# Sums of squares behind the output projection of a hybrid encoder layer: three whole token tiles per square, and a square root read from PSUM

## The chip, the cores and the metric

The kernel runs on 1 core of one Trainium2 chip. The metric is the device time of one execution in microseconds (us); the median of several runs is compared. Engines are named as in the profile: PE is TensorE, PEld its weight load, DVE VectorE, ACT ScalarE, POOL GpSimd, SP SyncE.

## The reference, cut to what matters

One layer with four token mixers and a gated feed-forward net over 272 tokens (16 meta tokens and 256 real ones) of width 2048, in float32. The stretch around the change is the norm behind the output projection:

```python
def rms_norm(x, g):
    xf = x.astype(jnp.float32)
    y = xf * lax.rsqrt(jnp.mean(xf * xf, axis=-1, keepdims=True) + EPS)
    return (y * g.astype(jnp.float32)).astype(x.dtype)
...
    mix = jnp.concatenate([y_a, y_b, y_c, y_d], axis=-1) @ w_out
    x = x + rms_norm(mix, g_mix_post)
    h = rms_norm(x, g_ffn_pre)
    gate = causal_dwconv(h @ ffn_w_gate, ffn_conv_w, ffn_conv_b)
    y = (jax.nn.silu(gate) * (h @ ffn_w_up)) @ ffn_w_down
    return x + rms_norm(y, g_ffn_post)
```

## The kernel before

Activations lie with features on the partitions and tokens along the free dimension. From the output projection on, 258 tokens are kept (2 that the causal convolution of the feed-forward net needs, and 256 real ones), cut into three segments by `SEGQ`: 2, 128 and 128 tokens. Every float32 weight tile is loaded from HBM by SP into one of three `raw` buffers, then split in halves of 128x1024 into a high part (`whi`, ACT, L176) and a low part (`wlo`, DVE, L182); a product is three matmuls (high by high, high by low, low by high: L237, L238, L239).

The output projection (L983 to L1012) makes 16 feature tiles in four groups of four. When a feature tile is done, ACT squares it from its PSUM bank and DVE adds the square to `ssum` (L964 to L970), and DVE multiplies it by the norm's gain into `mo` (`weigh`, L1001). The square of the last feature tile is not added: it stays apart as `slast` (L1005).

Then, from L1013 on, a stretch follows in which DVE and ACT run in the order in which their instructions are written (`manual_schedule`, L1014). PE is not held so: a list scheduler orders PE's instructions when the kernel is built, by its own idea of when operands are ready. `pin` (L107) ties one instruction behind the one that was written just before it for the same engine; it doesn't tie what is written later. The stretch is, in the order of writing:

- Line 1015 takes a PSUM bank `mrstd`, out of the pool `mx` with four banks.
- Lines 1017 and 1018: a quarter-wise split of a weight tile (`pieces`): four ACT copies, and the first of four DVE subtractions.
- Line 1019 calls `rstd_columns` (L271 to L286). It calls `square_sums` (L263 to L269): for `ssum`, then for `slast`, one matmul per segment (segments in the order 1, 2, 0) with the squares as the weights and a column of ones as the moving operand, so that the sums of 128, 128 and 2 tokens land as columns of a second bank of `mx`; 6 calls of matmul. Then POOL's memset of the tile `rs`, two DVE instructions that read the bank and compute mean + EPS (L283 for the segment of two tokens, L284 for the two of 128), and `rsqrt` (L288 to L296): ACT takes the root (L290), meanwhile DVE does one more subtraction of `pieces`, then the reciprocal (L293) and one Newton step (L294 to L296). Column `y` of the result is the reciprocal root, tokens on partitions.
- Line 1020: the remaining two subtractions of `pieces`.
- Lines 1057 to 1063: 32 PE transposes of `mo` (eight groups of four, `turned`, L1047 to L1051), each group into a bank of `mx`, the first five groups read by an ACT copy each (`keep`, L1054); in between, behind the fourth group, three PE transposes (`rstd_spread`, L298 to L299) that spread `y` along the tokens into `mrstd`.
- Lines 1065 to 1087: per feature tile k, DVE multiplies `mo` by `mrstd` (L1066), adds it to the residual stream (L1067), and ACT and DVE make the high and low part of the norm's input `hx` (L1070, L1071). The feed-forward matmuls begin with `hx` of feature tile 0.

Of the kernel before, what the change touches and what calls it, by code (L numbers as in the profile page):

```python
# [7 lines left out]
F32 = mybir.dt.float32  # L8
F32R = mybir.dt.float32r
AF = mybir.ActivationFunctionType  # L10
ALU = mybir.AluOpType
AX = mybir.AxisListType

P = 128
# [4 lines left out]
D = 2048  # L19
# [5 lines left out]
EPS = 1e-6  # L25
# [24 lines left out]
SEGQ = ((0, 2), (2, 128), (130, 128))  # L50
# [43 lines left out]
def hybrid_layer(ctx: ExitStack, tc, t):  # L94
    nc = tc.nc
    mm = nc.tensor.matmul
    act = nc.scalar.activation
    V = nc.vector
    G = nc.gpsimd

    const = ctx.enter_context(tc.tile_pool(name="const", bufs=1))
# [5 lines left out]
    pin = tc.keep_in_program_order  # L107
# [4 lines left out]
    def mix_ps():  # L112
        return pmix.tile([P, 512], F32, tag="mx", name="mx")
# [5 lines left out]
    sel_fox, sel_ssd, sel_tok = (cst[0:16, c:c + P] for c in (C_SELFOX, C_SELSSD, C_SELTOK))  # L119
    ones = const.tile([P, P], F32, name="ones")  # L120
    V.memset(ones, 1.0)

    def col(c):
        return cols[:, c:c + 1]
# [39 lines left out]
    def split_hi(i, half, n, pool=None, tiles=None):  # L164

        load(i)
        hi, lo = tiles or [(pool or wpool).tile([P, 1024], F32R, tag=tag, bufs=4, name=tag) for tag in ("whi", "wlo")]
        halves[i, half] = (hi, lo)
        steps = []
        cuts = [1024 * q // n for q in range(n + 1)] if (i, half) != (0, 0) else [0, 128, 512, 1024]  # L170
        for c in map(slice, cuts, cuts[1:]):
            if i:
                src = raws[i][:, 1024 * half + c.start:1024 * half + c.stop]
            else:
                src = packed(FIRST_W[2 * half + c.start // 512] + c.start % 512, c.stop - c.start)
            act(hi[:, c], src, AF.Copy)  # L176
            steps.append((lo[:, c], src, hi[:, c].bitcast(F32)))
        return iter(steps)

    def split_lo(steps, most=None):  # L180
        for _, (lo, src, hi) in zip(range(most or 16), steps):
            V.tensor_tensor(lo, src, hi, ALU.subtract)  # L182
# [80 lines left out]
    def square_sums(sq, segs, ps, g):  # L263
        n_seg = len(segs)
        order = [(j, i) for j in range(len(sq[g])) for i in (1, 2, 0)]
        for j, i in order:
            c0, n = segs[i]
            mm(ps[0:n, g * n_seg + i:g * n_seg + i + 1], sq[g][j][:, c0:c0 + n], ones[:, 0:1],
               start=g == 0 and (j, i) == order[0], stop=(j == len(sq[g]) - 1), skip_group_check=True)  # L269

    def rstd_columns(small, sq, scale, segs, ps, meanwhile=None, summed=False):  # L271

        n_seg, ng = len(segs), len(sq)
        if not summed:
            for g in range(ng):
                square_sums(sq, segs, ps, g)
        w = ng * n_seg
        v = small.tile([P, 4, 8], F32, tag="rs", bufs=2, name="rs")
        G.memset(v, 1.0)
        n0 = segs[0][1]  # L280
        pv = ps[:, 0:w].rearrange("p (g s) -> p g s", g=ng)
        vv = v[:, 0, 0:w].rearrange("p (g s) -> p g s", g=ng)
        V.tensor_scalar(vv[0:n0, :, 0:1], pv[0:n0, :, 0:1], scale, EPS, op0=ALU.mult, op1=ALU.add)  # L283
        V.tensor_scalar(vv[:, :, 1:n_seg], pv[:, :, 1:n_seg], scale, EPS, op0=ALU.mult, op1=ALU.add)  # L284
        rsqrt(v[:, 0, 0:w], v[:, 1, 0:w], v[:, 2, 0:w], v[:, 3, 0:w], meanwhile)
        return v[:, 2, 0:w]  # L286

    def rsqrt(v, s, y, z, meanwhile=None):  # L288

        pin(act(s, v, AF.Sqrt))  # L290
        if meanwhile:
            meanwhile()
        V.reciprocal(y, s)  # L293
        V.tensor_tensor(z, y, y, ALU.mult)  # L294
        V.scalar_tensor_tensor(z, z, -0.5, v, op0=ALU.mult, op1=ALU.mult)
        V.scalar_tensor_tensor(y, z, 1.5, y, op0=ALU.add, op1=ALU.mult)  # L296
# [661 lines left out]
    T = tst.enter_context(tc.tile_pool(name="resid", bufs=1, side="right"))  # L958
# [3 lines left out]
    ssum = T.tile([P, LQ], F32, name="ssum")  # L962
# [20 lines left out]
    for f4 in range(4):  # L983
# [13 lines left out]
        for f in range(4):  # L997
# [5 lines left out]
            if k == KT - 1:  # L1003
                slast = T.tile([P, LQ], F32, tag="tsq", bufs=2, name="slast")
# [11 lines left out]

    pieces = split_hi(FFN0 + 2, 0, 4)
    split_lo(pieces, 1)
    y = rstd_columns(T, [[ssum, slast]], 1.0 / D, SEGQ, mix_ps(), lambda: split_lo(pieces, 1))
    split_lo(pieces)  # L1020
    assert "early" in finished
    mixers.close()
# [175 lines left out]
    for k in range(FT):  # L1198
        i = base + k
# [28 lines left out]
    for b in range(2):  # L1228
# [20 lines left out]
        s, y, z = (st[:, c:c + 1] for c in (8, 9, 10))  # L1249
# [8 lines left out]
        if b:  # L1258
# [3 lines left out]
            for i, ps in enumerate(sums):  # L1262
                c0 = n_v + 256 * i
# [86 lines left out]
```

## Time and profile before

| | |
|---|---|
| median of 3 runs | 1126.2 us (1126.0 to 1126.65) |
| profiled execution, its own time | 1126.16 us |
| profiled execution, span from first to last instruction | 1124.0 us |
| PE busy | 1117.2 us |
| DVE busy | 721.9 us |
| ACT busy | 556.8 us |
| POOL busy | 30.9 us |
| mean granted PE clock | 0.999 of full speed |

The profile is of one execution. Busy time of PE counts matmuls whose ends are modelled, so that short waits between them can hide in it. A releaser (`<-`) is what ended an idle stretch. The span is 2.16 us shorter than the time of the same execution; that remainder lies outside the instructions.

### The profile page before, as it was taken

How to read it: one execution, taken by the hardware profiler on the slowest of the kernel's cores; microseconds unless marked ns; L12 is line 12 of the kernel's file. 1: busy time of each engine (PE TensorE's matmuls, PEld its weight loads, DVE VectorE, ACT ScalarE, POOL GpSimd, SP SyncE). 2: the span in 40 equal slices, each digit the busy share in tenths (PEclk: the TensorE clock that was granted, in tenths of full speed). 3: DMA queues.
4: the chain of work that ended last, by engine and by line, in shares of the span. 5: the costliest groups of instructions: out<-in, count | busy, mean ns of one | idle time of the engine just before them, and what ended most of it. 6: DMA issues, size and time to landing. Idle time of an engine off the chain costs nothing.

```text
span 1124.0 us, 18509 instructions
## 1 busy us (share of the span) xinstructions
PE 1117.2 (99%) x7590; PEld 1024.2 (91%) x7590; DVE 721.9 (64%) x1177; ACT 556.8 (50%) x820; POOL 30.9 (3%) x45
## 2 busy tenths in 40 slices
PE   9999999999999999999999999999999999999998
PEld 8999999999999999999899899998999888888886
DVE  7686676786656977656656566566665654455564
ACT  8343464573444656445444454445444544444453
POOL 0000011000000400000000000000000000000000
PEclk9999999999999999999999999999999999999999
DMA  9744434535556465555455545555555555555552
GB/s 322 254 168 173 153 132 160 170 141 178 185 180 214 183 220 193 187 186 184 157 203 183 183 180 190 185 188 187 188 187 187 188 187 191 192 201 200 190 187 75
DMA packets 32724, 208.30 MB, mean 185 GB/s; under 512 B 3696, under 2 KB 4736, under 8 KB 9344
## 3 DMA queue, kind: packets, MB, share of 16 engines
q1 hardware_dynamic: 30528, 198.17, 49.5%
q0 software_dynamic: 1680, 8.56, 2.3%
q8 instruction: 59, 0.97, 0.3%
q10 hardware_dynamic: 432, 0.39, 0.1%
q14 instruction: 25, 0.20, 0.0%
HBM read 204.99 MB, written 2.12 MB: 184 GB/s over the span
## 4 chain that ended last, share of the span: by engine, by line
PE 98%; DVE 1%; DMA 0%; ACT 0%; issue 0%; SPq 0%; DVEq 0%
PE acc L237 16%; PE acc L239 16%; PE acc L238 16%; PE mx L232 15%; PE mx L233 7%; PE acc L1194 4%; PE acc L1195 4%; PE acc L1193 4%; PE mx L1194 3%; PE mx L1195 3%; PE mx L1193 3%; PE mx L1226 1%; PE mx L620 1%; PE mx L237 1%; PE mx L238 1%; PE mx L239 1%
## 5 line engine op out<-in xcount | busy, mean ns | idle before, releaser
L182 DVE TENSOR_TENSOR wlo<-raw,whi 128x1024 fp32r<-128x1024 f32 (+2 forms) x369 | 445.4, 1212 | 321.4 <-ACT whi L176 315.5
L176 ACT ACTIVATE whi<-raw 128x1024 fp32r<-128x1024 f32 (+2 forms) x369 | 383.3, 1047 | 450.1 <-PE acc L238 194.5
L232 PE MATMUL mx<-hx,whi 128*128 128x512 f32 x704 | 249.2, 397 | 0.0
L233 PE MATMUL mx<-hx,wlo 128*128 128x256 f32 x704 | 197.7, 281 | 0.0
L239 PE MATMUL acc<-hx,wlo 128*128 128x258 f32 x688 | 195.0, 284 | 0.0
L238 PE MATMUL acc<-hx,whi 128*128 128x258 f32 x688 | 193.8, 282 | 0.0
L237 PE MATMUL acc<-hx,whi 128*128 128x258 f32 x688 | 193.1, 283 | 0.0
L232 PEld LDWEIGHTS mx<-hx,whi 128*128 128x128 f32 x704 | 132.5, 188 | 31.8
L237 PE MATMUL acc<-xh,whi 128*128 128x272 f32 (+3 forms) x512 | 151.5, 298 | 0.6 <-ACT whi L176 0.6
L238 PE MATMUL acc<-xl,whi 128*128 128x272 f32 (+3 forms) x512 | 146.6, 287 | 0.0
L239 PE MATMUL acc<-xh,wlo 128*128 128x272 f32 (+3 forms) x512 | 145.2, 287 | 0.4 <-DVE wlo L182 0.4
L233 PEld LDWEIGHTS mx<-hx,wlo 128*128 128x128 f32 x704 | 132.5, 188 | 0.0
L238 PEld LDWEIGHTS acc<-hx,whi 128*128 128x128 f32 x688 | 130.2, 189 | 0.3 <-DVE hx L1071 0.2
L237 PEld LDWEIGHTS acc<-hx,whi 128*128 128x128 f32 x688 | 129.7, 189 | 0.6
L239 PEld LDWEIGHTS acc<-hx,wlo 128*128 128x128 f32 x688 | 129.5, 188 | 0.0
L237 PEld LDWEIGHTS acc<-xh,whi 128*128 128x128 f32 x512 | 96.6, 189 | 7.2 <-issue 5.0
L238 PEld LDWEIGHTS acc<-xl,whi 128*128 128x128 f32 x512 | 96.9, 189 | 1.2 <-issue 0.7
L239 PEld LDWEIGHTS acc<-xh,wlo 128*128 128x128 f32 x512 | 95.8, 189 | 0.9 <-DVE wlo L182 0.9
L1195 PE MATMUL acc<-wlo,yh 128*128 128x512 f32 x176 | 68.5, 389 | 0.0
L1194 PE MATMUL acc<-whi,yl 128*128 128x512 f32 x176 | 68.5, 389 | 0.0
L1193 PE MATMUL acc<-whi,yh 128*128 128x512 f32 x176 | 68.5, 389 | 0.0
L1193 PE MATMUL mx<-whi,yh 128*128 128x512 f32 x160 | 62.2, 389 | 0.0
(379 smaller groups left out, 1499.3 us busy)
## 6 DMA issues: line engine op xcount, KB each, us to landing
raw<-w_gate SPq DMA_DIRECT2D x44, 1024.0 KB, 4.8
raw<-w_up SPq DMA_DIRECT2D x44, 1024.0 KB, 4.7
raw<-w_down SPq DMA_DIRECT2D x44, 1024.0 KB, 4.8
raw<-w_in SPq DMA_DIRECT2D x32, 1024.0 KB, 4.9
raw<-w_out SPq DMA_DIRECT2D x16, 1024.0 KB, 4.9
xT<-xT POOLq DMA_DIRECT2D x1, 2064.0 KB, 12.0
raw<-w_in SPq DMA_DIRECT2D x4, 512.0 KB, 7.8
yT<-x_tok POOLq DMA_DIRECT2D x1, 2048.0 KB, 8.1
```

Of the source, the lines that this page charges most:

```text
L176: act(hi[:, c], src, AF.Copy)
L182: V.tensor_tensor(lo, src, hi, ALU.subtract)
L232: mm(accs[f][:, :2 * n], hi[:, c], both(kts[k]), start=st, stop=False)
L233: mm(accs[f][:, n:2 * n], lo[:, c], xh, start=False, stop=en)
L237: mm(out, hi[:, c], xh[:, o:], start=st, stop=False)
L238: mm(out, hi[:, c], xl[:, o:], start=False, stop=False)
L239: mm(out, lo[:, c], xh[:, o:], start=False, stop=en)
L620: mm(ps[:, j * nk:(j + 1) * nk], q[r, h0 // 2 + j, qc:qc + P], k[r, h0 // 2 + j, 0:nk], start=True, stop=True)
L1193: mm(o, yh, hi[:, c], start=(k == 0), stop=False)
L1194: mm(o, yl, hi[:, c], start=False, stop=False)
L1195: mm(o, yh, lo[:, c], start=False, stop=(k == FT - 1))
L1226: mm(po[1][q], y, w[:, c], start=False, stop=(k == FT - 1 and w is lo))
```

## The change

A tile `eps` of one column is set to EPS at the start. Behind the output projection the call of `rstd_columns` is replaced: the sums are taken over three tiles of 128 tokens that begin at tokens 0, 2 and 130 (the first overlaps the second; of its result only the first two tokens are used), first the three of `ssum`, then the three of `slast`, each matmul pinned behind the one before it. ACT takes the root directly from the bank of the sums, with `eps` as its bias and 1/D as its scale; one DVE instruction writes mean + EPS for the Newton step. The tile `rs` is no longer set on POOL beforehand. The remaining uses of `rstd_columns` are as they were.

```diff
     ones = const.tile([P, P], F32, name="ones")
     V.memset(ones, 1.0)
+    eps = const.tile([P, 1], F32, name="eps")
+    V.memset(eps, EPS)
...
     pieces = split_hi(FFN0 + 2, 0, 4)
     split_lo(pieces, 1)
-    y = rstd_columns(T, [[ssum, slast]], 1.0 / D, SEGQ, mix_ps(), lambda: split_lo(pieces, 1))
+
+    psq = mix_ps()
+    for sq in (ssum, slast):
+        for i, c0 in enumerate((0, 2, 130)):
+            pin(mm(psq[:, i:i + 1], sq[:, c0:c0 + P], ones[:, 0:1], start=(i == 0 and sq is ssum),
+                   stop=sq is slast, skip_group_check=True))
+    v = T.tile([P, 4, 3], F32, tag="rs", name="rs")
+    s, y, z = (v[:, i, :] for i in (1, 2, 3))
+    pin(act(s, psq[:, 0:3], AF.Sqrt, bias=eps, scale=1.0 / D))
+    V.tensor_scalar(v[:, 0, :], psq[:, 0:3], 1.0 / D, EPS, op0=ALU.mult, op1=ALU.add)
+    split_lo(pieces, 1)
+    V.reciprocal(y, s)
+    V.tensor_tensor(z, y, y, ALU.mult)
+    V.scalar_tensor_tensor(z, z, -0.5, v[:, 0, :], op0=ALU.mult, op1=ALU.mult)
+    V.scalar_tensor_tensor(y, z, 1.5, y, op0=ALU.add, op1=ALU.mult)
     split_lo(pieces)
```

## Rows read from the trace of the kernel before

**Rows 1.** The page: its span, and busy time, share and instructions of each engine.
```profile
span 1124.0 us, 18509 instructions
...
PE   1117.2 (99%) x7590; PEld 1024.2 (91%) x7590; DVE 721.9 (64%) x1177; ACT 556.8 (50%) x820; POOL 30.9 (3%) x45
```

**Rows 2.** All waits of PE in the span: in total, times, longest (us).
```profile
PE mx L358 <- DVE ones L121: 1.1, 1, 1.1
PE acc L237 <- ACT whi L176: 0.6, 1, 0.6
PE acc L239 <- DVE wlo L182: 0.4, 2, 0.2
PE mx L299 <- DVE rs L296: 0.2, 1, 0.2
```

**Rows 3.** By stretch: length, busy time (count) of PE, PEld, DVE, ACT, POOL, clock, DMA.
```profile
366.60:372.20 5.60, 5.39 (x51) 5.02 (x49) 4.30 (x16) 4.25 (x11) 0.56 (x1) 1.00 0.82 293
...
420.00:800.00 380.00, 380.00 (x2684) 356.25 (x2683) 240.50 (x347) 186.05 (x245) 0.00 (x0) 1.00 0.53 186
```

**Rows 4.** Chain of work that ended last, in order of time: start, length, what.
```profile
370.07 0.55 PE mx L299 x3
370.62 1.78 PE mx L1050 x16
```

**Rows 5.** Timeline of PE's weight loads: start, length, line, out<-in, count [idle before].
```profile
366.61 0.63 PEld L268 LDWEIGHTS mx<-ones,ssum 128*128 128x128 f32 x6
367.28 0.53 PEld L1050 LDWEIGHTS mx<-cst,mo 128*128 128x128 f32 x5
367.77 0.63 PEld L268 LDWEIGHTS mx<-ones,slast 128*128 128x128 f32 x6
368.44 1.19 PEld L1050 LDWEIGHTS mx<-cst,mo 128*128 128x128 f32 x11
370.04 0.34 PEld L299 LDWEIGHTS mx<-cst,rs 2*128 2x128 f32 x3 [0.42 <-issue]
...
372.14 0.53 PEld L237 LDWEIGHTS acc<-hx,whi 128*128 128x128 f32 x4
```

**Rows 6.** One line's instructions: ns shortest, median and longest, first and last start, forms.
```profile
L268 PEld LDWEIGHTS mx<-ones,slast x6: 81/191/192, 367.8 to 368.3; 128*128 128x128 f32 x4, 128*2 128x2 f32 x2
```

**Rows 7.** Timeline of ACT in the stretch of the change.
```profile
367.03 0.37 ACT L1005 ACTIVATE slast<-acc 128x258 f32<-128x258 f32 x1
...
368.92 0.20 ACT L290 ACTIVATE rs<-rs 128x3 f32<-128x3 f32 x1 [1.22 <-DVE rs L284]
369.03 2.66 ACT L1054 ACTIVATE xtok<-mx 128x512 f32<-128x512 f32 x5
371.58 0.50 ACT L1070 ACTIVATE hx<-xT,cols 128x258 fp32r<-128x258 f32 x1
```

**Rows 8.** Timeline of DVE in the stretch of the change.
```profile
367.43 0.48 DVE L1001 TENSOR_SCALAR mo<-acc,cols 128x258 f32<-128x258 f32 x1 [0.36 <-ACT slast L1005]
368.62 0.15 DVE L283 TENSOR_SCALAR rs<-mx 2x1 f32<-2x1 f32 x1 [0.70 <-PE mx L268]
...
368.76 0.40 DVE L182 TENSOR_TENSOR wlo<-raw,whi 128x256 fp32r<-128x256 f32 x1
369.16 0.18 DVE L293 RECIPROCAL rs<-rs 128x3 f32<-128x3 f32 x1
...
369.76 0.16 DVE L296 SCALAR_TENSOR_TENSOR rs<-rs 128x3 f32<-128x3 f32 x1
369.84 0.75 DVE L182 TENSOR_TENSOR wlo<-raw,whi 128x256 fp32r<-128x256 f32 x2
370.65 0.42 DVE L1066 TENSOR_TENSOR mo<-mo,mx 128x258 f32<-128x258 f32 x1
```

**Rows 9.** ACT by line and shape, 1100 to 1124 us: count, busy, mean ns.
```profile
L1250 ACT ACTIVATE fst<-fst 128x1 f32<-128x1 f32 x2 | 0.6, 296 | 0.0
```

**Rows 10.** Timeline of DVE at the start of the kernel.
```profile
3.19 0.36 DVE L375 TENSOR_SCALAR xh<-first 128x272 fp32r<-128x272 f32 x1 [1.99 <-DMA first<-first]
```

## The prediction

> **What bounds the kernel now.** I read the page's engine shares first: PE is busy 1117.2 us of a span of 1124.0 us, so a gain can only come out of PE's work or out of PE's few idle moments [rows 1]. All waits of PE that the profile names come to 2.3 us, and one of them, L299 waiting for the end of the Newton step, lies in the stretch of the change [rows 2]. The table by stretch says the same: between 366.6 and 372.2 us PE lacks 0.21 us of being always busy, and in the long feed-forward stretch from 420 to 800 us it lacks nothing, DMA at 0.53 of its share [rows 3]. So whatever moves the first feed-forward matmul at 372.14 us [rows 5] is carried unchanged to the end: nothing behind it has slack to swallow a shift or a wait for weights to undo it.
>
> The stretch itself is read in three timelines side by side. PE: six sums of `ssum` from 366.61, five transposes from 367.28, six sums of `slast` from 367.77, eleven transposes from 368.44, then 0.42 us without a weight load before the three spreads of `y` at 370.04 [rows 5]. DVE: the bank is read at 368.62, reciprocal at 369.16, last Newton step from 369.76 to 369.92, and the first product with the spread root at 370.65 [rows 8]. ACT: `slast` from 367.03 to 367.40, root at 368.92, five copies in a row until 371.69, overlapping by a little the first `hx` at 371.58 [rows 7]. The spreads wait for the Newton step, not for PE: the path is slast, its sums, root, reciprocal, Newton, spreads (370.07 plus 0.55), the 16 transposes behind them, feed-forward [rows 4]. From the load of the first spread to the first feed-forward load it is 2.10 us, filled twice over: by PE's transposes (until 372.40 in the chain) and by the product, the sum and `hx`, which ends at 372.08 [rows 4, 5, 7]. So a gain counts only if it reaches the spreads, and there it counts one to one.
>
> **Part 1: three sums in place of six, twice.** Six loads of `ssum` take 367.28 − 366.61 = 0.67 us, 0.11 us each [rows 5]. Three fewer ahead let PE go on at 366.95. What comes next is not in the diff: the pin holds each sum behind the previous one, but transposes, written later and not pinned, may still be listed in between, as five of them are now. Five take 0.49 us, 0.10 us each [rows 5]. With n of them, the first sum of `slast` loads at 366.95 + 0.10 n, and not before `slast` is there. That ends at 367.40 [rows 7]; from the end of the last Newton step at 369.92 to the spreads' load it is 0.12 us [rows 5, 8], so I take 367.52. Up to n = 5 the wait decides; n = 6 gives 367.55, n = 8 gives 367.75, hardly earlier than now. More than 8 don't fit: `mx` has four banks, one each for `mrstd` and the sums, and two groups of four fill the others.
>
> Now the bank is read 368.62 − 367.77 = 0.85 us after the first load [rows 5, 8]. Three sums fewer take away 0.33, leaving 0.52; but the last one is now a whole tile, whose load takes 0.19 us where that of two tokens takes 0.08 [rows 6], so 0.52 to 0.63, and I take 0.60. The sums are then readable at 368.12 to 368.15 (n up to 6) or 368.35 (n = 8): 0.47 to 0.50, or 0.27 us, sooner. I have no row that says which n the list takes; three sums of 0.11 us are three transposes' worth of room more than now, which points from 5 towards 8, so I take 6 to 8.
>
> **Part 2: the root from the bank.** The two DVE instructions ahead of the root go off the root's path, which starts 0.30 us after the sums now (368.62 to 368.92) [rows 7, 8]. But the root was not what the reciprocal waited for: it ends at 369.12, and DVE reaches the reciprocal at 369.16 straight from the subtraction of 0.40 us at 368.76 [rows 7, 8]. The reciprocal stands 0.54 us behind the first read of the bank, by DVE's own work.
>
> The new DVE instruction, mean + EPS, reads the same bank as the root. Two readers of one bank are ordered here: L1001 on DVE and L1005 on ACT both only read the last accumulator, and L1001 sat 0.36 us until L1005 was over, starting 0.03 us behind it [rows 7, 8]. The root is written first, so DVE waits for it. Behind the waiting instruction on DVE stand the subtraction of 0.40 us and then the reciprocal. The root's price is not in the trace: without bias and scale operands it is 0.20 us [rows 7], with a bias tile, at the end of the kernel, 0.296 us [rows 9]. The second is nearest, since `eps` is a tile. So from the sums to the reciprocal: 0.30 root, 0.03 until DVE starts, 0.07 for mean + EPS (the spacing of the two that it replaces, 0.14 us for two), 0.40 subtraction: 0.80 us in place of 0.54, that is 0.26 us later [rows 7 to 9]. With the root at 0.20 us it is 0.16 us later.
>
> [...] If both could read at once, the reciprocal would stand 0.47 us behind the sums and the whole would be 0.33 us better than my sum. [...]
>
> **The rest.** The setting of `eps` falls on DVE before 3.19 us, where DVE waits 1.99 us for the first DMA [rows 10]; nothing. The dropped memset is on POOL, busy 3% [rows 1]; nothing. The root now frees ACT for its copies earlier than 369.03 [rows 7], and they are then paced by the transposes; ACT is not late. The two subtractions behind the Newton step end at 370.59 now, 0.03 us ahead of the spreads [rows 4, 8]; they move with the Newton step. The subtractions also free a weight buffer for SP's next load; that moves by the same tenths, and PE waits for no load behind this point [rows 2]. If PE idles a little longer ahead of `slast`, the clock is no worry that rows show: 0.42 us of idle in this stretch left it at 1.00 [rows 3, 5].
>
> **The sum.** For n up to 6: 0.47 to 0.50 sooner, 0.26 later, net 0.21 to 0.24 us gained. For n = 8: 0.27 − 0.26, nothing. In between, 0.15 us. With the profiled execution's own time of 1126.16 us that is 1126.0; it stands 0.04 us under the median of 1126.2, so the median becomes 1126.05, rounded to 1126.0.
>
> **Rivals.**
> First, a clearer gain: DVE does not wait for the root, or the root is short. For: ACT sat 1.22 us idle ahead of the root, so nothing there can hold it up [rows 7]. Against: L1001's wait. Without the wait the gain is 0.33 + 0.22 = 0.55 us, with a root of 0.20 us it is 0.32: 1125.6 to 1125.9.
>
> Second, slower: the spreads are listed behind more transposes. They stand behind 16 of 32 now, and PE idles before them [rows 5], because the fifth group's bank comes free only with ACT's copies. With the root earlier by 368.92 − 368.15 = 0.77 us, these copies, some 0.53 us apart (2.66 for five) [rows 7], free banks sooner, and a list that fills idle room may put two more groups ahead of the spreads. The fifth group needs the end of the second copy, about 369.5, the sixth that of the third, about 370.05; eight transposes then end near 370.5, and the spreads load there in place of 370.04: 0.46 us slower, 1126.6. One group more ends near 369.95 and gives 1126.1. It decides from the second extra group on. Against: only if the list expects `y` later than it now does.
>
> Third, the change doesn't do what it says: the sums end up no earlier, with n = 8 and one more wait, or the list of PE comes out otherwise somewhere else. In the first form it is 0 to 0.1 us slower, 1126.2 to 1126.3. In the second nothing here prices it; what speaks against it is that before this stretch only a memset of a column is new and behind it PE is full [rows 3].
>
> **How the numbers follow.** The forecast 0.55 (1125.9 to 1126.25), the clear gain 0.18, the slower spreads 0.15, the third 0.12. The range reaches from the clear gain to the slower spreads, with the 0.2 to 0.45 us by which single runs lie under and over the median (1126.0 to 1126.65): 1125.3 to 1126.8. Bounds for faster and slower are 0.2%, 2.25 us, about what a measurement of this kernel can tell from no change; all worked-out cases are inside, and only a list that changes elsewhere could leave it: 0.03 faster, 0.94 same, 0.03 slower.
>
> **What would show it.** In the timeline of PE: three sums, some transposes, three sums, each sum 0.11 us apart. On ACT the root at 368.1 to 368.4 with a length near 0.30 us. On DVE mean + EPS behind the root's end, waiting for ACT, and the reciprocal about 0.80 us behind the root's start. The first feed-forward load at 371.9 to 372.1, and the same shift in the span. It is wrong if mean + EPS starts with the root (then 0.33 us better), if the spreads load later than 370.04, or if the span moves by more than 1 us, since no part of this stretch holds that much.

## The result: 1132.11 us, 5.9 us slower, and where the time went

The changed kernel takes 1132.11 us (1131.97 to 1132.25, five runs) against 1126.2 us (1126.0 to 1126.65): a ratio of 1.0052, 95% interval 1.0041 to 1.0063. The forecast was 1126.0 us with a range up to 1126.8.

The page of the changed kernel, its span and engine shares, answers to [rows 1]:

```profile
span 1130.5 us, 18504 instructions
...
PE 1123.2 (99%) x7590; PEld 1023.3 (91%) x7590; DVE 722.5 (64%) x1177; ACT 557.2 (49%) x820; POOL 30.4 (3%) x44
```

PE has the same 7590 matmul rows as before and is busy 6.0 us longer, while its named waits grow only from 2.3 us [rows 2] to 2.9 us: the matmuls themselves stand further apart. Since the rows are the same in number and, from stage to stage, in kind, the two traces can be laid beside each other matmul by matmul. In the table below the stages are cut at the starts of five matmuls: the first sum of `ssum`, the first feed-forward matmul, the first and the last matmul of the down projection, and the last matmul of the kernel. The numbers are differences of those starts in us.

```
                         first sum at  the stretch  gate and up  down     behind it
before                   366.73        5.43         503.65       239.50   3.95
with the change          366.34        5.63         503.65       246.11   3.94
```

The stretch that the change is about loses 0.20 us. Gate and up projection take the same to the hundredth. The down projection, of which the diff says nothing, loses 6.61 us. The stages up to the first sum are 0.39 us shorter; that start lay between 366.16 and 366.99 us in the runs of the longer table below.

The view by stretch, first two lines of the kernel before, then two of the changed one (stretch, its length, busy time and count of PE, PEld, DVE, ACT, POOL, granted clock, DMA share, GB/s):

```profile
500.00:800.00 300.00, 300.00 (x2111) 280.87 (x2110) 186.55 (x265) 143.58 (x186) 0.00 (x0) 1.00 0.52 183
950.00:1000.00 50.00, 50.00 (x222) 41.42 (x221) 26.21 (x28) 22.31 (x28) 0.00 (x0) 1.00 0.55 192
```

```profile
500.00:800.00 300.00, 300.00 (x2111) 280.95 (x2110) 186.71 (x266) 143.59 (x186) 0.00 (x0) 1.00 0.52 183
950.00:1000.00 50.00, 50.00 (x216) 40.13 (x216) 24.67 (x28) 21.69 (x27) 0.00 (x0) 1.00 0.54 190
```

PE is busy for the whole of each stretch in both, at the same clock of 1.00. What differs is the count: 2111 against 2111 in the gate and up projections, but 222 against 216 in 50 us of the down projection. "Busy" hides it; the count in brackets shows it.

Four matmuls in a row there, PE's timeline, first of the kernel before, then of the changed one:

```profile
950.39 0.39 PE L1195 MATMUL mx<-wlo,yh 128*128 128x512 f32 x1
950.62 0.39 PE L1193 MATMUL mx<-whi,yh 128*128 128x512 f32 x1
950.84 0.39 PE L1194 MATMUL mx<-whi,yl 128*128 128x512 f32 x1
951.07 0.39 PE L1195 MATMUL mx<-wlo,yh 128*128 128x512 f32 x1
```

```profile
950.28 0.40 PE L1211 MATMUL acc<-wlo,yh 128*128 128x512 f32 x1
950.52 0.39 PE L1209 MATMUL acc<-whi,yh 128*128 128x512 f32 x1
950.75 0.40 PE L1210 MATMUL acc<-whi,yl 128*128 128x512 f32 x1
950.98 0.39 PE L1211 MATMUL acc<-wlo,yh 128*128 128x512 f32 x1
```

From start to start it is 226.7 ns before and 233.3 ns after, as means over 960 matmuls; 1056 matmuls times 6.6 ns is 7.0 us, of which 6.6 appear, since the last 96 stepped unevenly already before.

The stretch itself, timelines of PEld, ACT and DVE of the changed kernel, answering to [rows 5, 7, 8]:

```profile
366.22 0.75 PEld L1025 LDWEIGHTS mx<-ones,ssum 128*128 128x128 f32 x6
366.81 0.62 PEld L1066 LDWEIGHTS mx<-cst,mo 128*128 128x128 f32 x5
367.40 0.75 PEld L1025 LDWEIGHTS mx<-ones,slast 128*128 128x128 f32 x6
367.98 1.27 PEld L1066 LDWEIGHTS mx<-cst,mo 128*128 128x128 f32 x11
369.85 0.33 PEld L301 LDWEIGHTS mx<-cst,rs 2*128 2x128 f32 x3 [0.60 <-ACT xtok L1070]
...
371.95 0.53 PEld L239 LDWEIGHTS acc<-hx,whi 128*128 128x128 f32 x4
```

```profile
368.27 0.26 ACT L1029 ACTIVATE rs<-mx,eps 128x3 f32<-128x3 f32 x1 [0.95 <-PE mx L1025]
```

```profile
368.56 0.16 DVE L1030 TENSOR_SCALAR rs<-mx 128x3 f32<-128x3 f32 x1 [1.04 <-ACT rs L1029]
368.64 0.42 DVE L184 TENSOR_TENSOR wlo<-raw,whi 128x256 fp32r<-128x256 f32 x1
368.97 0.17 DVE L1032 RECIPROCAL rs<-rs 128x3 f32<-128x3 f32 x1
...
369.57 0.16 DVE L1035 SCALAR_TENSOR_TENSOR rs<-rs 128x3 f32<-128x3 f32 x1
...
370.47 0.42 DVE L1082 TENSOR_TENSOR mo<-mo,mx 128x258 f32<-128x258 f32 x1
```

Two things are to be seen. Each square still has six loads and five transposes still stand between: three sums of a float32 square are six rows, before and after, and nothing was taken off PE. And mean + EPS waits 1.04 us, in the end for ACT's root, from the start of which the reciprocal is 0.70 us away (368.27 to 368.97).

### The profile page after: what moved, and what is told of

Read it like the earlier page. It is cut to its first block, busy times and chain, and to the rows that moved or that the text cites. A ratio compares the mean times of both kernels' runs of the same rounds, so it can differ in the third digit from the quotient of the medians.

```text
span 1130.5 us, 18504 instructions
## 1 busy us (share of the span) xinstructions
PE 1123.2 (99%) x7590; PEld 1023.3 (91%) x7590; DVE 722.5 (64%) x1177; ACT 557.2 (49%) x820; POOL 30.4 (3%) x44
## 4 chain that ended last, share of the span: by engine, by line
PE 98%; DVE 0%; DMA 0%; ACT 0%; issue 0%; SPq 0%
PE acc L239 16%; PE acc L241 16%; PE acc L240 16%; PE mx L234 15%; PE mx L235 7%; PE acc L1210 4%; PE acc L1209 4%; PE acc L1211 4%; PE mx L1210 3%; PE mx L1209 3%; PE mx L1211 3%; PE mx L1242 1%; PE mx L622 1%; PE mx L239 1%; PE mx L241 1%; PE mx L240 1%
```

## The experiments

The suspect came from the diff itself: `eps` is a new tile. It holds one column, but it stands in the pool `const` and takes 32 bytes of every partition there, and all pools allocated behind `const` from the same side move by 32 bytes: `raw`, `whi`, `wlo` and the activations that stand on that side, `hx` among them. `yh` and `yl`, at the other end of the memory, don't move. In the built kernels `whi` begins at byte 37344 of the partition before and at 37376 after, `yh` at 219104 in both. In the down projection `whi` and `wlo` are the moving operands and `yh` and `yl` the weights, so their distance changes by 32 bytes.

**The tile and the code, taken apart.** First the change without the move:

```diff
-    eps = const.tile([P, 1], F32, name="eps")
+    root_eps = const.tile([P, 2], F32, name="root")
+    root, eps = root_eps[:, 0:1], root_eps[:, 1:2]
     V.memset(eps, EPS)
...
-    root = const.tile([P, 1], F32, name="root")
```

> The change as it is, but eps is the second column of the tile root, which already has 32 bytes, so that no other tile moves. Theory 'place' (the 6.6 us come from the 32 bytes by which the new tile eps moves all tiles behind it, the split weights whi and wlo among them, while yh and yl stay where they were): a matmul of the down projection steps every 226.7 ns again in place of 233.3 ns, and the time falls to that of the kernel before plus the 0.2 us that the stretch of the change loses, 1126.2 to 1126.6 us. Rival 'code' (the new sums or the root from the bank do it): 233.3 ns and 1132 us as with the change.

Then the move without the change, on the kernel before:

```diff
     V.memset(ones, 1.0)
+    pad = const.tile([P, 8], F32, name="pad")
+    V.memset(pad, EPS)
```

> The kernel before with nothing but an unused tile of 32 bytes behind ones, set once. Theory 'place': 233.3 ns per down matmul, 1131.6 to 1132.1 us. Rival 'code': 226.7 ns and 1126.2 us.

Measured: 1126.26 us with eps in root, a ratio of 1.000 to the kernel before (0.999 to 1.001), and 1132.33 us with the unused tile, 1.0054 (1.0037 to 1.0071). The stretch from 950 to 1000 us, first with eps in root, then with the unused tile:

```profile
950.00:1000.00 50.00, 50.00 (x222) 41.42 (x221) 26.21 (x28) 21.87 (x27) 0.00 (x0) 1.00 0.55 193
```

```profile
950.00:1000.00 50.00, 50.00 (x216) 40.17 (x215) 24.68 (x28) 21.83 (x27) 0.00 (x0) 1.00 0.53 190
```

The 222 and 216 matmuls go with the tile and not with the code: the step is 226.7 ns in the first run and 233.3 ns in the second. What the diff means to do is worth nothing that the times can tell, and the whole loss that they can tell is made by 32 bytes of room. "Place" stands, "code" falls.

**Place or distance.** Does it count where `whi` lies, for instance on a multiple of 64 bytes, or how far it lies from the weights? The tile made 64 bytes long:

```diff
-    eps = const.tile([P, 1], F32, name="eps")
+    eps = const.tile([P, 16], F32, name="eps")[:, 0:1]
```

> The change with eps as a tile of 64 bytes, so that tiles move by 64 in place of 32 bytes. If what counts is whether whi and wlo begin on a multiple of 64 bytes (32 beyond one is fast, on one is slow): 226.7 ns, 1126.4 us. If it is the distance in bytes between the moving operand and the weights over a longer period: another step than 226.7, somewhere between 226 and 240 ns, 1126 to 1139 us.

And `yh`, `yl` moved alone, in the kernel before, by another distance at each step k:

```diff
-        yh = Y.tile([P, SEQ], F32R, tag="yh", bufs=LAST + 1, name="yh")
-        yl = Y.tile([P, SEQ], F32R, tag="yl", bufs=LAST + 1, name="yl")
+        o = 8 * (k % 16)
+        yh = Y.tile([P, SEQ + P], F32R, tag="yh", bufs=LAST + 1, name="yh")[:, o:o + SEQ]
+        yl = Y.tile([P, SEQ + P], F32R, tag="yl", bufs=LAST + 1, name="yl")[:, o:o + SEQ]
```

> The kernel before with yh and yl placed 32*(k mod 16) bytes into longer tiles, k being the step of the down projection; whi and wlo stay. If the distance between moving operand and weights counts, the step of the matmuls goes with k mod 16: 226.7 ns at 0, 233.3 ns at 15 (the distance that the change has), others between. If only the place of the moving operand counts: 226.7 ns for every k and 1126.2 us.

Measured: 64 bytes give 1128.63 us (1.0022, interval 1.0012 to 1.0031) and 228.9 ns: neither the old step nor the worse one, so a multiple of 64 is not the rule. The view by stretch of that run:

```profile
950.00:1000.00 50.00, 50.00 (x220) 41.02 (x219) 25.67 (x29) 21.83 (x27) 0.00 (x0) 1.00 0.54 190
```

With the moved weights (1131.6 us, one run) the step follows k mod 16. Mean start-to-start of the matmuls within a step k of the down projection, k = 1 to 39; the two or three k of the same offset agree within 0.1 ns:

```
yh, yl moved by (bytes)   0     32    64    96    128   160   192   224
step (ns)                 226.7 233.1 233.4 233.9 233.5 233.4 229.3 233.3
moved by                  256   288   320   352   384   416   448   480
step (ns)                 226.7 233.1 233.4 233.9 233.5 233.4 229.3 233.3
```

The pattern repeats after 256 bytes. Moving the weights by 224 is the same distance as moving the operand by 32 (233.3 ns both), and by 192 the same as moving it by 64 (229.3 against 228.9 ns). So place alone falls. The test from the other side is the change as it is, with the tile `eps`, where the distance is restored by moving the weights too:

```diff
-        yh = Y.tile([P, SEQ], F32R, tag="yh", bufs=LAST + 1, name="yh")
-        yl = Y.tile([P, SEQ], F32R, tag="yl", bufs=LAST + 1, name="yl")
+        yh = Y.tile([P, SEQ + P], F32R, tag="yh", bufs=LAST + 1, name="yh")[:, 8:8 + SEQ]
+        yl = Y.tile([P, SEQ + P], F32R, tag="yl", bufs=LAST + 1, name="yl")[:, 8:8 + SEQ]
```

> The change as it is, its tile eps too, with yh and yl 32 bytes further into longer tiles, so that the distance to whi and wlo is again that of the kernel before while all absolute places differ from it. Theory 'distance': 226.7 ns per down matmul and 1125.4 to 1126.1 us. If the place of whi and wlo alone counts: 233.3 ns and 1132 us.

Measured: 1125.73 us (1.000, 0.999 to 1.001), 226.7 ns, and in the view by stretch:

```profile
950.00:1000.00 50.00, 50.00 (x222) 41.40 (x221) 26.22 (x28) 22.56 (x28) 0.00 (x0) 1.00 0.55 196
```

Of `whi`, `wlo`, `yh` and `yl` none lies where it did in the kernel before; the distance is the same modulo 256 bytes, and so is the step. That shows the cause: the distance between the moving operand and the weights. By what mechanism the distance acts is not shown. (`raw`, from which the split weights are made, moves with them in these runs; the run with all three below tells the two apart.)

**How fine, and which load.** Two looks at what the distance does. In steps of 4 bytes (as above with `o = 48 + k % 32`):

> The kernel before with yh and yl placed at 192 + 4*(k mod 32) bytes into longer tiles: distances of 64 bytes less to 60 bytes more than a multiple of 256 bytes, in steps of 4. Theory 'distance' (moving operand minus weights, modulo 256 bytes): k mod 32 = 16 has distance 0 and 226.7 ns, 0 has 229.3, 8 has 233.3, 24 has 233.1. Open is what lies between: if only whole blocks of 32 or 64 bytes count, levels; if it is exact, a narrow dip around one value, perhaps below 226.7 ns. If distance is not the cause: no pattern over k mod 32.

And `yl` alone moved by 32 bytes (as in the run before, with 0 for `yh` and 8 for `yl`, on the kernel before):

> The kernel before with yl alone 32 bytes further, yh as it was. The matmuls go yh by whi, yl by whi, yh by wlo. If the load of the next weights is what meets the moving stream of the running matmul, one step in three grows, that from yh by whi to yl by whi, in which yl is loaded: 233 ns there and 226.7 ns in the others, 1128.3 us. If it is the weights in use: the step from yl by whi to yh by wlo grows. If place alone counts: none grows, 1126.2 us.

Measured, steps of 4 bytes (1130.58 us, one run; offsets relative to a multiple of 256):

```
offset   -64   -60   -56   -52   -48   -44   -40   -36   -32   -28   -24   -20   -16   -12   -8    -4
ns       229.4 233.3 230.7 226.7 232.2 236.2 232.0 233.3 233.3 226.7 231.2 231.8 228.3 233.3 233.3 226.7
offset   0     4     8     12    16    20    24    28    32    36    40    44    48    52    56    60
ns       227.6 232.3 230.7 229.8 233.4 232.6 231.0 235.0 233.1 234.4 233.3 230.3 233.3 233.4 233.0 230.6
```

No levels of 32 or 64 bytes: 226.7 ns comes back at -52, -28 and -4, 24 bytes apart, 236 ns is the worst, and nothing is below 226.7. Offset 0 has 227.6 here and 226.7 where its neighbours in time had other offsets, so the offset alone does not settle a step to the last ns; what else does was not tried.

With `yl` alone moved the time is 1132.63 us (one run), not the 1128.3 us that was expected. PE's timeline of that run:

```profile
951.28 0.40 PE L1193 MATMUL mx<-whi,yh 128*128 128x512 f32 x1
951.52 0.39 PE L1194 MATMUL mx<-whi,yl 128*128 128x512 f32 x1
951.74 0.40 PE L1195 MATMUL mx<-wlo,yh 128*128 128x512 f32 x1
951.98 0.40 PE L1193 MATMUL mx<-whi,yh 128*128 128x512 f32 x1
```

In means, the step from L1193 to L1194, in which `yl` is loaded, is 239.2 ns, the next 228.0, and that from L1195 back to L1193 is 232.8 ns, although no operand of it has moved against another. The load of the moved tile is hit hardest, which fits the first theory, but one of the two untouched steps grows by 6.6 ns as well, which it doesn't. Steps are coupled; how is left open.

**The stretch of the change.** The 0.20 us that the code itself loses should be DVE's wait for the root. With eps in root, the subtraction is written ahead of the bank's read:

```diff
-    V.tensor_scalar(v[:, 0, :], psq[:, 0:3], 1.0 / D, EPS, op0=ALU.mult, op1=ALU.add)
     split_lo(pieces, 1)
+    V.tensor_scalar(v[:, 0, :], psq[:, 0:3], 1.0 / D, EPS, op0=ALU.mult, op1=ALU.add)
```

> The change with eps in the tile root (nothing moves), and the DVE subtraction between the bank's read and the reciprocal written ahead of the read: it then fills the time in which DVE waits for the root. Theory 'two readers of a bank take turns': the reciprocal comes 0.1 us behind the root in place of 0.44, the stretch is 0.3 us shorter than with the change, 1125.8 to 1126.0 us. If DVE waits for the sums and not for the root: no change against the run with eps in root, 1126.2 us.

Measured: 1126.06 us (1.000, 0.999 to 1.001); the times can't tell such a step, the trace can. Its timelines of PEld, ACT and DVE:

```profile
366.64 0.76 PEld L1025 LDWEIGHTS mx<-ones,ssum 128*128 128x128 f32 x6
...
369.94 0.33 PEld L302 LDWEIGHTS mx<-cst,rs 2*128 2x128 f32 x3 [0.26 <-ACT xtok L1070]
...
372.04 0.54 PEld L240 LDWEIGHTS acc<-hx,whi 128*128 128x128 f32 x4
```

```profile
368.70 0.26 ACT L1029 ACTIVATE rs<-mx,root 128x3 f32<-128x3 f32 x1 [0.96 <-PE mx L1025]
```

```profile
368.99 0.16 DVE L1031 TENSOR_SCALAR rs<-mx 128x3 f32<-128x3 f32 x1 [1.04 <-ACT rs L1029]
369.07 0.17 DVE L1032 RECIPROCAL rs<-rs 128x3 f32<-128x3 f32 x1
```

The read still starts 0.03 us behind the root's end, with nothing else for DVE to do: it waits for the root and not for the sums. The reciprocal now stands 0.37 us behind the root's start in place of 0.70, and the stretch takes 5.30 us in place of 5.63 (5.43 before).

**Together.** A version that has the change, the distance and the order, and that also brings the split weights in the pool `E` to a distance of a multiple of 256. These are the split weights of two of the last four steps, not of all four: 48 of the last 96 matmuls. They stood at a distance of 128 bytes in the kernel before; a longer `diag` in their pool moves them by 96 bytes, and the move of the weights by 32 does the rest:

```diff
-            diag = E.tile([P, P], F32, name="diag")
+            diag = E.tile([P, P + 24], F32, name="diag")[:, 0:P]
```

> Three things together: the change with yh and yl moved by 32 bytes as in the run after_y32, the subtraction ahead of the bank's read as in the run sub_first, and the split weights of the last four steps of the down projection (tiles of their own, at a distance of 128 bytes to yh and yl in the kernel before) at a distance of a multiple of 256 bytes. Theory 'distance': about 48 of the last 96 matmuls step 226.7 ns in place of some 233, 0.3 us; the subtraction 0.3 us; after_y32 stood at 1125.73 us, so 1125.1 us. If the last four steps are slow for another reason: 1125.4 us.

Measured: 1125.03 us (1124.62 to 1125.25), a ratio of 0.9989 to the kernel before, interval 0.9980 to 0.9998. The stages cut as above, in us:

```
                         first sum at  the stretch  gate and up  down     behind it
before                   366.73        5.43         503.65       239.50   3.95
with the change          366.34        5.63         503.65       246.11   3.94
eps in root              366.98        5.64         503.67       239.50   3.95
unused tile, 32 bytes    366.16        5.43         503.67       246.11   3.95
64 bytes                 366.99        5.63         503.68       241.71   3.94
change, y moved by 32    366.26        5.63         503.66       239.66   3.95
subtraction first        366.77        5.30         503.76       239.50   3.95
all three                366.52        5.29         503.77       239.15   3.94
```

The last 96 matmuls step 226 to 227 ns, each one of them, where they stepped between 224 and 238 ns in the kernel before; in the run with the change and `yh`, `yl` moved by 32, the same matmuls still stepped 232.0 ns in the mean. Between that run and this one `raw`, `yh` and `yl` kept their places and only tiles of `E` moved (the code differs in the order of two instructions far ahead of it), so it is the distance of the split weights that counts. This version is the fastest measured here. Of its 1.1 us the profiles account for 0.14 us in the stretch and 0.35 us in the down projection; the two spans differ by only 0.5 us (1123.5 against 1124.0; the profiled execution took 1125.25 us), so the rest is not explained by them. In the two runs with the subtraction first, gate and up take 0.1 us longer: matched matmul by matmul, 0.34 us of gain over the run with eps in root shrinks to 0.23 us at 374 to 377 us, where a weight load of the feed-forward waits 0.3 us for DVE's `hx` in place of 0.2 us.

**Why the gate and up projections were spared.** There `hx` is the moving operand and the split weights are the weights, and both stand on the side that moves: in the built kernels `hx` begins at byte 139712 before and at 139744 after, 32 bytes further like `whi`. So the change alters no distance there, and their 503.65 us stay. Whether distance counts in these stages is another question. The rows of `hx` are 1032 bytes apart, so each feature tile has another distance. With rows 1280 bytes (5 times 256) apart, each begun 16 k bytes later, the four blocks and both parts of a feature tile share one distance:

```diff
-    hx = HP.tile([P, 2, KT, LQ], F32R, name="hx")
...
+    hx = HP.tile([P, 2, KT, 320], F32R, name="hx")
...
+    def hx_of(half, k, c0=0):
+        o = 4 * k
+        return hx[:, half, k, o + c0:o + LQ]
...
```

> The kernel before with the rows of hx, the moving operand of the gate and up projections, 1280 bytes apart in place of 1032 and begun 16*k bytes into the row, k being the feature tile: the distance to the weights is then the same for all four feature blocks and for the high and the low part, and goes through a whole period of 256 bytes with k. Theory 'distance': the step of these matmuls depends on k, as that of the down matmuls on its k; the mean over k stays near that of the kernel before, 1125 to 1130 us. If only the down projection is touched by distance: the same step for every k.

Measured: 1128.84 us, one run, and by stretch:

```profile
500.00:800.00 300.00, 300.00 (x2097) 280.32 (x2097) 185.92 (x265) 143.46 (x185) 0.00 (x0) 1.00 0.52 184
```

14 matmuls fewer than the 2111 of before in 300 us; gate and up take 505.99 us. The layout counts there too, but neither expectation fits. The step of the gate's matmuls (128x258) went only from 118.6 to 121.4 ns over the sixteen k, with no pattern like that of the down projection, and is the same in the mean, 120.1 against 120.2 ns before. The loss lies in the matmuls of the up projection: 236.4 against 234.4 ns for those of 128x512, 120.4 against 118.8 ns for those of 128x256. What sets these steps was not followed up, so the pattern of the down projection is not to be carried over to them.

## Why the prediction was wrong, point by point

**What bounds the kernel: right, but for 0.1 us.** PE is the bound and a shift is carried: gate and up took 503.65 to 503.77 us in all runs of the table, wherever the stretch before them ended; the 0.1 us by which the two runs with the subtraction first stand out goes with the wait for `hx` at 374 us, so a gain in the stretch is not carried quite unchanged. The same sentence should have warned: where PE is full, the step of its matmuls is the time, and whatever changes that step by 3% in a fifth of the kernel outweighs everything in a stretch of 5 us.

**Part 1, fewer sums: wrong, by a misread row.** The step that failed is "three sums in place of six". The timeline's x6 for `ssum` is three calls of a float32 matmul with two rows each; the code has one call per segment in both versions, and the count of calls in the description of the kernel, six for both squares, stands against x6 twice in the rows. No sum was removed. The sums are readable 2.05 us after the first load (366.22 to 368.27) against 2.01 before [rows 5, 8]; the 0.27 to 0.50 us that they were to come sooner are not there, and 0.04 us are lost. The list, with five transposes between and not the 6 to 8 that were taken, is that of before.

**Part 2, the root from the bank: right in kind, a little too dear.** Mean + EPS waits for the root and starts 0.03 us behind its end, as L1001 did behind L1005 [rows 7, 8]. Both write into the tile `rs`, but that alone would not order them: in the kernel before ACT and DVE write different parts of `hx` at the same time (ACT from 376.41 to 376.92 us, DVE from 376.02 to 376.66 us). From the sums to the reciprocal it is 0.70 us, predicted 0.80, before 0.54: the root takes 0.26 us (0.30 taken, 0.20 to 0.296 given as bounds), and the subtraction leads to the reciprocal in 0.33 rather than 0.40. The root with a bias tile from SBUF, at the end of the kernel before, took 0.296 us [rows 9], but the two roots differ in shape, three columns against one, and no run here takes the same root from both: what the bank as a source is worth is not shown. From the sums to the reciprocal the order of two readers of a bank costs 0.16 us (0.70 against 0.54), and with the sums 0.04 us later in part 1 the stretch lost 0.20 us where 0.15 were to be won.

**The rest: the step that cost 6.6 us.** "The setting of `eps` falls on DVE before 3.19 us ... nothing" is right about the memset and wrong about the tile: the term put at nothing measured 6.6 us, all of it in the down projection (239.50 to 246.11 us). The price of an instruction was looked for, not that of the room it takes. The third rival came nearest in that something could change outside the stretch, but it named the order of PE's list, and it was given no price. The order did change in one place, without a price: one matmul of the up projection stands at 376 us in place of 384 us. The rows are the same 7590, and from 416 to 870 us the two traces lie a constant 0.18 us apart.

**The rivals.** The clearer gain needed DVE not to wait for the root; it waits. The slower spreads needed more transposes ahead of them; there are 16, as before. The range and the chance of 0.94 for no change rested on cases that all lie inside 2.25 us, because all of them lay inside the stretch. The sign named for being wrong, a span that moves by more than 1 us since no part of the stretch holds that much, did hold: it pointed out of the stretch.

## What to carry to other kernels

Of a new tile, ask not only who writes and reads it but what it pushes aside: compare the addresses of the operands of the costliest matmuls, moving operand against weights, before and after an edit, modulo 256 bytes. This is shown here for 128x512 matmuls that each load 128x128 weights (226.7 ns a step, 233.3 ns with 32 bytes more); the gate's 128x258 matmuls did not follow the pattern (118.6 to 121.4 ns over the sixteen k). When a kernel changes by a constant amount per matmul in a stage that nobody touched, count matmuls per stretch first, then repeat the edit's memory without its code. To make such operands safe against edits elsewhere, place both in pools whose distance is fixed on purpose, as `hx` and the split weights happen to be here, rather than one at each end of the memory.

## What the runs showed of the hardware

The step of a 128x512 matmul with its own weight load was 226.7 ns at best and 236 ns at worst, as means over a step k within one execution, by the distance of moving operand and weights, at a granted clock of 0.999 to 1.00. The pattern repeats after 256 bytes (the same to 0.1 ns in steps of 32 bytes); inside, it is fine down to 4 bytes (233.3 ns at an offset of -8, 226.7 ns at -4). Why the steps are coupled when `yl` alone is moved (239.2, 228.0 and 232.8 ns), no run shows.

Through which part of the chip the distance acts on the step, no run here shows either.
